# FFN1 of a macaron layer: the weight ring's hi halves moved by 64 bytes, and the down projections cut into two pieces of 384 tokens

## The chip, the cores and the metric

The kernel runs on one NeuronCore of a Trainium2 chip. The metric is the device time of one execution in microseconds (us): median 1112.95 us of three runs (1112.82 to 1113.49). Lower is better. TensorE multiplies matrices and accumulates in PSUM banks of 512 fp32 columns; VectorE (DVE), ScalarE (ACT) and GpSimd (POOL) work elementwise; SyncE (SP) issues the loads.

## What is computed

One hybrid backbone layer over 512 latent and 256 context tokens, model width 1024, feed-forward width 2816:

```
def swiglu(h, w1, w3, w2):
    return (jax.nn.silu(h @ w1) * (h @ w3)) @ w2

def ffn_sublayer(h_in, shift, scale, gate, norm_w, w1, w3, w2):
    h = modulate(rms_norm(h_in, norm_w), shift, scale)
    return h_in + 0.5 * gate * swiglu(h, w1, w3, w2)

x   = ffn_sublayer(x, ...norm1, ffn1)        # FFN1, latent tokens
ctx = ffn_sublayer(ctx, ...norm1, ffn1)      # FFN1, context tokens
...                                          # attention and spatial gating
x   = ffn_sublayer(x, ...norm3, ffn2)        # FFN2, latent tokens only
```

The nine shifts, scales and gates come from `silu(c) @ w_ada + b_ada`. All of it is fp32.

## The kernel before, in words

Each fp32 operand is held as two parts: hi (rounded to the multiplier's format) and lo (the rest). One product of a weight and an activation is three matmuls on TensorE, `mm3`: hi weight by hi activation, hi weight by lo, lo weight by hi. In the rows of the profile the weights are `oph` and `opl`, the normalised input of FFN1 is `hh` and `hl`, and the product silu·gate, the input of the down projection, is `gh` and `gl`.

FFN1 handles all 768 tokens together, ordered as two groups of 384 (256 latent and 128 context tokens each). The 22 feature tiles of 128 are made in turn. Tiles 0 and 1 are made in the prologue, 2 and 3 plainly (two 384-column halves), and 4 to 21 by a Winograd scheme of seven half-size products instead of eight (`Winograd.unit`; its operands are slices of hh, hl and the sums `u2`, `u3`, `u4`). Every product there is 12 matmuls of 384 columns. The down projection comes in four chunks of 5, 5, 6 and 6 feature tiles: the first three stand behind feature tiles 6, 10 and 16 (`DOWN1`, `after1`), the last one behind tile 21 (`last_mm`, in two halves of 384 already).

The weights come by DMA into raw tiles. ScalarE casts 512 columns to hi, VectorE subtracts to get lo; a pair of them is one of five slots (`OPS`) of a ring (`Stream.pair`). `Flow` keeps the order: `slot` first runs the evacuations left over from the product before, then gives back its ring slots, refills the ring and runs a filler (in the down stages two dot products of the modulation on VectorE, `ada_step`). From slot to slot the order on every engine is that in which the code is written.

`down_thirds` makes one output tile of 128 features at a time from three pieces of 256 tokens: the latent tokens of group 0, those of group 1, and the 2 × 128 context tokens. The first two fill one PSUM bank, the third a second one. VectorE adds the first bank into x (`evac_part`) while the third piece runs, and the second bank in the next slot. The last product ahead of each such stage (`cut`) has its last three matmuls split into 128 and 256 columns.

PSUM has eight banks: four under the name `mm`, and four that are either four `one` or two pairs `big`. A Winograd tile takes four `mm` when its number is even, four `one` when it is odd.

Each tile has a fixed place in SBUF. Of a partition's row, counted modulo 128 bytes: hh, hl, the sums u2 to u4 and all ten ring tiles start at 64; the g tiles of FFN1 start at 0. In FFN2 the ring is at 64 too, and most token blocks at 0.

Of the kernel before, what the change touches and what calls it, by code (L numbers as in the profile page):

```python
# [17 lines left out]
P = 128  # L18
# [10 lines left out]
CHUNKS1 = [5, 5, 6, 6]  # L29
DOWN1 = [6, 10, 16]  # L30
# [6 lines left out]
BLOCKS = 2  # L37
RAWS = 3
OPS = 5
GA, GB = (0, 384), (384, 384)  # L40

COL_B, COL_N1, COL_N2, COL_N3 = 0, 72, 80, 88
COL_QA, COL_KVA, COL_BS, COL_QN, COL_KN, COL_C = 96, 98, 99, 107, 108, 109
# [74 lines left out]
class Stream:  # L118


    def __init__(self, nc, raw_pool, op_pool, op_bufs, dram):
        self.pin = lambda i: i
        self.nc, self.raw_pool, self.op_pool, self.op_bufs, self.dram = nc, raw_pool, op_pool, op_bufs, dram

    def block(self, src, i, pool=None):
# [15 lines left out]
        return dst  # L141

    def pair(self):
        return [self.op_pool.tile([P, 512], F32R, tag=f"op{p}", bufs=self.op_bufs, name=f"op{p}_{self.nc.next_id()}") for p in "hl"]

    def operand(self, src, eng=None):
        return self.split([t[:, : src.shape[1]] for t in self.pair()], src, eng)
# [26 lines left out]
def layer_kernel(ctx: ExitStack, tc: tile.TileContext, xT, wfirst, wst, wada, wuq, wkpe, cols, wrope, vnw, rope, out):  # L174
    nc = Core(tc)
# [66 lines left out]
    fctx = ExitStack()  # L242
    fp = fctx.enter_context(tc.tile_pool(name="ffn1", bufs=2))
    cb = fp.tile([P, 2, D], F32, tag="cb", bufs=1, name="cb")
    gp = fctx.enter_context(tc.tile_pool(name="ffn1g", bufs=2))
    hfctx = ExitStack()
    hfp = hfctx.enter_context(tc.tile_pool(name="hf", bufs=1))
# [435 lines left out]
    gt = {}  # L683
# [60 lines left out]
        for p in range(2 * n):  # L744
            flow.todo.append(lambda p=p: want(p))

    def down_thirds(flow, f0, n, step):
        pairs, gone = [], 0
        for dt in range(NK):
            flow.slot(lambda: step(dt))  # L750
            while 4 * len(pairs) < dt * n + n:
                pairs.append(flow.take())
            pts = [mm(), mm()]
            for t in range(3):
                o = pts[0][:, 256 * t : 256 * t + 256] if t < 2 else two(pts[1][:, :256])
                for fi in range(n):
                    q, u = divmod(dt * n + fi, 4)
                    g = [a[:, 384 * t : 384 * t + 256] if t < 2 else two(a)[:, :, 256:384] for a in gt[f0 + fi]]
                    mm3(nc, o, [a[:, u * P : u * P + P] for a in pairs[q]], g, fi == 0, fi == n - 1)
                if t == 1:  # L760
                    evac_part(pts[0], dt, "lat", 512)

            def last(pt=pts[1], dt=dt):
                evac_part(pt, dt, "ctx", 256)
                yield

            flow.pend = [last()]
            flow.spent = (dt * n + n) // 4 - gone
            gone += flow.spent
# [36 lines left out]
        nc.scalar.copy(dst[0], src)  # L806
        nc.vector.tensor_sub(dst[1], src, dst[0].bitcast(F32))

    def prod(pb, A, Bk, n, first=True, cut=False):
        for i in range(4):  # L810
            s = slice(i * P, i * P + P)
            parts = ((256, n), (0, 256)) if cut and i == 3 else ((0, n),)
            for a, b in parts:
                mm3(nc, pb[:, a:b], (A[0][:, s], A[1][:, s]), (Bk[0][:, i, a:b], Bk[1][:, i, a:b]), first and i == 0,
                    i == 3 and a == 0, not first)

    class Winograd:

# [71 lines left out]
        def product(self, bank, blk, first, pend, step=None, cut=False):  # L890
            flow = self.flow
            a = flow.take()
            flow.slot(step or (lambda: None))
            prod(bank, a, self.blocks[blk], self.n, first, cut)
            flow.spent = 1
            flow.pend = [pend] if pend else []

        def open(self, f, step, f0=None, splits=()):
            n = self.n
            banks = [one() if f % 2 else mm() for _ in range(4)]  # L900
            banks = [banks[i] for i in (0, 1, 3, 2)]
            p1 = self.tmp("p1", n)

            def evac():
                nc.scalar.copy(p1, banks[0][:, :n])
                yield
                if f == f0:
                    for split_g in splits:
                        split_g()

            self.product(banks[0], "B11", True, evac(), step)
            return banks, p1

        def unit(self, f, hd, step):
            n, v = self.n, nc.vector
            banks, p1 = hd
            X, Y, Z, W = (b[:, :n] for b in banks)
            u2, u3 = self.tmp("u2", n), self.tmp("u3", n)
            sl = self.tmp("sl", n, self.sl_bufs)
            gh, gl = self.g_tile(f)  # L920

            def ev_sl():
                nc.scalar.activation(sl, X, AF.Silu)
                yield

            def ev_u2():
                v.tensor_add(u2, Y, p1)
                yield

            def ev_u2z():  # L930
                v.tensor_add(u2, Y, p1)
                yield
                v.tensor_add(Z, Z, u2)

            def ev_u3():
                nc.scalar.copy(u3, W)
                v.tensor_add(u3, Z, u3)
                yield

            def ev_lo():  # L940
                v.tensor_add(W, W, u2)
                v.tensor_mul(W, W, sl)
                yield
                g_split(W, gh[:, :n], gl[:, :n])

            def ev_hi(seeded=False):
                if not seeded:
                    v.tensor_add(Z, Z, u2)
                yield
                nc.scalar.activation(Z, Z, AF.Silu)  # L950
                v.tensor_mul(Z, Z, u3)
                g_split(Z, gh[:, n:], gl[:, n:])

            def ev_u3a():
                v.tensor_add(u3, W, u2)
                yield

            def ev_u3b():
                v.tensor_add(u3, Z, u3)
                yield  # L960

            nxt = None
            if f == self.late or f + 1 == NF:
                self.product(banks[1], "T2", True, ev_u2(), lambda: step(f, 0))
                self.product(banks[3], "T3", True, ev_u3a(), lambda: step(f, 1))
                self.product(banks[0], "B21", False, ev_sl(), lambda: step(f, 2))
# [12 lines left out]
            self.product(banks[2], "B22", False, ev_hi(seeded), cut=n > 256 and f in DOWN1)  # L979
            return nxt  # L980

        def run(self, flow, f0, after, step=lambda f, i: None, opening=None, splits=()):
# [6 lines left out]
            flow.slot()  # L989
            other_banks()  # L990

    def evac_part(pt, dt, g, n):
        sel, which = (lat, 0) if g == "lat" else (cxt, 1)
        v = sel(x, dt)
        nc.vector.scalar_tensor_tensor(v, two(pt[:, :n]), mod_g[0][which][:, dt : dt + 1], v, ALU.mult, ALU.add)

    ada = ada_rest()

    def ada_step(n=1):
        for _ in range(n):  # L1000
            next(ada, None)
# [3 lines left out]

    def after1(flow, f):
        for ci in ends1(f):
            down_thirds(flow, starts1[ci], CHUNKS1[ci], lambda dt: ada_step(2))

    def ada_up(f, i):  # L1010
        if f == NPLAIN1:
# [56 lines left out]
                yield  # L1068

    flow = Flow(OPS)  # L1070
    for f in range(NFIRST):
        g_tile(f)
    wino = Winograd(gp, 384, U_UP1, blocks, g_tile, 1, 4)
# [180 lines left out]
        pt = last_mm(0, dt)  # L1254
    assert next(consts, None) is None and len(lastp) == 2 * lastn
    hA = hB = None
    inw = [[] for _ in range(3)]

    def in_want(i, w):
# [670 lines left out]
    flat = lambda T: [t.rearrange("p k c -> p (k c)") for t in T]  # L1930
    sA, sB = SsqAcc(t3, 256, nc.vector), SsqAcc(t3, 256, nc.vector)
    homes = [[wpool.tile([P, 1024], F32R, bufs=1, name=f"w{w}{p}") for p in "hl"] for w in range(2)] + [flat(T3), flat(T4)]
    wpool.tile([P, 16], F32, bufs=1, name="pad_w")

    def w_hi(w):
        for i in (0, 512):
# [269 lines left out]
```

## Time and profile before

| | us |
|---|---|
| median of three runs | 1112.95 |
| span of the profiled execution (the only time that its profile gives) | 1110.9 |
| TensorE busy (its weight loads) | 1104.4 (1056.4) |
| VectorE, ScalarE, GpSimd busy | 882.9, 537.7, 308.9 |
| prologue with feature tiles 0 and 1 | 0 to 60.6 |
| feature tiles 2 to 21 and three down stages | 60.6 to 487.2 |
| of it the down stages | 139.9 to 180.7, 239.1 to 280.0, 367.5 to 416.5 |
| last down chunk of FFN1 | 487.2 to 538.1 |
| projections, attention, gating | 538.1 to about 770 |
| FFN2 | about 770 to 1110.9 |

A group row names line, engine, operation, output and inputs, shape and count, then busy time, the mean time of one in ns, and idle time before them. A row of the chain of waits gives the start, the time and the count of work that followed on without another releaser. Times of single matmuls include the part in which they overlap their neighbours; the distance from one start to the next is shorter. The granted TensorE clock is 1.0 throughout.

### The profile page before, as it was taken

The numbers are of one execution on the slowest core, as the hardware profiler recorded it, in microseconds if no ns is written. First come the engines' busy times: TensorE is split into PE (matmuls) and PEld (weight loads), VectorE is DVE, ScalarE is ACT, GpSimd is POOL, SyncE is SP. The second block draws the span as 40 slices with busy tenths as digits, with TensorE's granted clock in tenths as the row PEclk, the third lists the DMA queues.
The fourth block names the chain that finished last, engine by engine and source line by source line (L and its number), as shares of the span: only waits on it lengthen the run. The fifth ranks groups of instructions, "written<-read, shape, count | busy, mean of one in ns | idle before, by whom it ended". The sixth has DMA issues, their size and how long they took to land.

```text
span 1110.9 us, 19724 instructions
## 1 busy us (share of the span) xinstructions
PE 1104.4 (99%) x7616; PEld 1056.4 (95%) x7616; DVE 882.9 (79%) x1590; ACT 537.7 (48%) x1110; POOL 308.9 (28%) x268
## 2 busy tenths in 40 slices
PE   9999999999999999999999999999999999999998
PEld 7899999999999999999988889999999989898997
DVE  5779898888888778866756899978886969696884
ACT  6545422431444214444755559985554536353451
POOL 0003303312243023300008427750014425152330
PEclk9999999999999999999999999999999999999999
DMA  9721353344334765312242211003221422333302
GB/s 357 272 65 50 123 169 127 114 135 151 120 107 151 239 200 190 114 59 79 86 134 94 76 38 34 26 21 114 77 96 57 144 86 83 108 115 114 114 2 95
DMA packets 35678, 125.96 MB, mean 113 GB/s; under 512 B 3712, under 2 KB 10624, under 8 KB 30976
## 3 DMA queue, kind: packets, MB, share of 16 engines
q1 hardware_dynamic: 35440, 124.63, 33.1%
q8 instruction: 60, 0.98, 0.4%
q14 instruction: 34, 0.28, 0.1%
q10 hardware_dynamic: 144, 0.06, 0.0%
HBM read 122.58 MB, written 2.10 MB: 112 GB/s over the span
## 4 chain that ended last, share of the span: by engine, by line
PE 94%; DVE 3%; DMA 1%; ACT 1%; issue 0%; POOL 0%; SPq 0%; ACTq 0%; DVEq 0%; POOLq 0%
PE mm L59 55%; PE one L59 19%; PE big L59 8%; PE mm L169 2%; PE mm L170 2%; PE mm L168 2%; PE big L596 1%; PE mm L581 1%; DMA scale<-wada 1%; PE big L170 1%; PE big L168 1%; PE big L169 1%; PE mm L330 1%; DMA x<-xT 0%; DVE opl L59 0%
## 5 line engine op out<-in xcount | busy, mean ns | idle before, releaser
L59 DVE TENSOR_TENSOR opl<-block,oph 128x512 fp32r<-128x512 f32 x216 | 190.0, 888 | 29.8 <-ACT oph L59 27.4
L59 POOL TENSOR_TENSOR block<-block 128x512 f32<-128x512 f32 x69 | 104.1, 1509 | 380.2 <-DVE opl L59 377.6
L59 ACT CAST oph<-block 128x512 fp32r<-128x512 f32 x216 | 133.9, 622 | 109.0 <-PE mm L59 81.9
L59 PE MATMUL mm<-gh,oph 128*128 128x256 f32 (+2 forms) x573 | 176.7, 308 | 0.0
L59 PE MATMUL mm<-gl,oph 128*128 128x256 f32 (+2 forms) x573 | 176.4, 308 | 0.0
L59 PE MATMUL mm<-gh,opl 128*128 128x256 f32 (+2 forms) x573 | 176.4, 308 | 0.0
L59 DVE SCALAR_TENSOR_TENSOR x<-mm,g,x 128x512 f32<-128x512 f32 (+2 forms) x136 | 79.1, 601 | 47.4 <-PE mm L59 47.1
L59 PEld LDWEIGHTS mm<-gl,oph 128*128 128x128 f32 x573 | 107.6, 188 | 5.6
L59 PEld LDWEIGHTS mm<-gh,oph 128*128 128x128 f32 x573 | 107.6, 188 | 5.5
L59 PEld LDWEIGHTS mm<-gh,opl 128*128 128x128 f32 x573 | 107.6, 188 | 5.4
L59 ACT CAST oph<-raw 128x512 fp32r<-128x512 f32 x113 | 68.7, 621 | 77.5 <-PE mm L59 53.0
L59 DVE TENSOR_TENSOR opl<-raw,oph 128x512 fp32r<-128x512 f32 x113 | 77.6, 702 | 11.6 <-ACT oph L59 10.9
L59 POOL TENSOR_TENSOR block<-s,block 128x512 f32<-128x512 f32 x35 | 46.6, 1331 | 130.4 <-DVE opl L59 129.6
L59 PE MATMUL mm<-hh,oph 128*128 128x384 f32 (+2 forms) x195 | 65.2, 334 | 0.0
L59 PE MATMUL mm<-hl,oph 128*128 128x384 f32 (+2 forms) x195 | 64.8, 333 | 0.0
L59 PE MATMUL mm<-hh,opl 128*128 128x384 f32 (+2 forms) x195 | 64.8, 332 | 0.0
L59 DVE SCALAR_TENSOR_TENSOR junk<-raw,cb 128x1024 bf16<-128x1024 f32 x48 | 62.2, 1309 | 0.0
L59 POOL TENSOR_TENSOR s<-block 128x512 f32<-128x512 f32 x34 | 55.6, 1636 | 10.6 <-DMA block<-wst 10.6
L59 DVE SCALAR_TENSOR_TENSOR raw<-raw,cb 128x1024 f32<-128x1024 f32 x32 | 42.2, 1323 | 7.9 <-DMA raw<-wada 7.9
L59 PE MATMUL one<-hl,oph 128*128 128x384 f32 x144 | 48.1, 334 | 0.0
L59 PE MATMUL one<-hh,oph 128*128 128x384 f32 x144 | 48.1, 334 | 0.0
L59 PE MATMUL one<-hh,opl 128*128 128x384 f32 x144 | 48.1, 334 | 0.0
(711 smaller groups left out, 3382.8 us busy)
## 6 DMA issues: line engine op xcount, KB each, us to landing
raw<-wst SPq DMA_DIRECT2D x77, 512.0 KB, 3.9
block<-wst SPq DMA_DIRECT2D x36, 1024.0 KB, 5.0
raw<-wada SPq DMA_DIRECT2D x56, 512.0 KB, 4.3
scale<-wada SPq DMA_DIRECT2D x16, 512.0 KB, 9.0
x<-xT SPq DMA_DIRECT2D x5, 512.0 KB, 6.3
raw<-wfirst SPq DMA_DIRECT2D x8, 256.0 KB, 9.1
out<-x SPq DMA_DIRECT2D x7, 256.0 KB, 2.3
raw<-wuq SPq DMA_DIRECT2D x2, 384.0 KB, 5.1
```

The source lines that it names most:

```text
L59: return lambda *a, **k: self.tc.keep_in_program_order(f(*a, **k))
L168: nc.tensor.matmul(out, lh, rh, start=first, stop=False, skip_group_check=more)
L169: nc.tensor.matmul(out, lh, rl, start=False, stop=False, skip_group_check=more)
L170: nc.tensor.matmul(out, ll, rh, start=False, stop=last, skip_group_check=more)
L330: pin(nc.tensor.matmul(pa[q, :P], scw[:, kt, 2 - 2 * w : 34 - 2 * w], units[d][w][:, kt * P : kt * P + P], start=w == 0 and kt < 4, stop=w ...
L581: pin(nc.tensor.matmul(o, l[:, c], r, start=k == 0 and m == 0 and w == 0, stop=k == NK - 1 and m == 2, skip_group_check=True))
L596: pin(nc.tensor.matmul(two(pbs[i]), ops[k][lo][:, i * P : i * P + P], lat(r, k), start=False, stop=k == NK - 1 and m == 2, skip_group_chec ...
```

## The change

The five ring slots become two tiles, one for hi and one for lo, of which slots are slices. The hi tile is 16 elements (64 bytes) longer. With `st.lower = 16`, set ahead of feature tile 2's weights and unset behind FFN1, a hi slice starts 16 elements lower, which is 0 modulo 128 bytes; lo slices stay at 64. Three pads move what follows: the ring's own, one ahead of FFN1's g tiles (which now start at 64), and a longer one ahead of FFN2's kept weights (which stay at 64, 128 bytes lower). `down_thirds` becomes `down_halves`: two pieces of 384 tokens, one for each group, in the two banks of one `big`; both additions into x run in the next slot. The split of the last matmuls (`cut`) goes. Even Winograd tiles of FFN1 use two `big` pairs, odd ones the four `mm`.

```
     def pair(self):
-        return [self.op_pool.tile([P, 512], F32R, tag=f"op{p}", bufs=self.op_bufs, ...) for p in "hl"]
+        if not self.ring:
+            self.op_pool.tile([P, 48], F32, name="pad_ring")
+            self.ring = [self.op_pool.tile([P, 512 * self.op_bufs + n], F32R, name=f"op{p}") for p, n in (("h", 16), ("l", 0))]
+        o = self.pairs % self.op_bufs * 512
+        self.pairs += 1
+        return [t[:, a : a + 512] for t, a in zip(self.ring, (o + 16 - self.lower, o))]
...
+    fp.tile([P, 16], F32, bufs=1, name="pad_g")
     gp = fctx.enter_context(tc.tile_pool(name="ffn1g", bufs=2))
...
-    def down_thirds(flow, f0, n, step):
+    def down_halves(flow, f0, n, step):
...
-            pts = [mm(), mm()]
-            for t in range(3):
-                o = pts[0][:, 256 * t : 256 * t + 256] if t < 2 else two(pts[1][:, :256])
+            pt = big()
+            for h in range(2):
                 for fi in range(n):
                     q, u = divmod(dt * n + fi, 4)
-                    g = [a[:, 384 * t : 384 * t + 256] if t < 2 else two(a)[:, :, 256:384] for a in gt[f0 + fi]]
-                    mm3(nc, o, [a[:, u * P : u * P + P] for a in pairs[q]], g, fi == 0, fi == n - 1)
-                if t == 1:
-                    evac_part(pts[0], dt, "lat", 512)
-            def last(pt=pts[1], dt=dt):
-                evac_part(pt, dt, "ctx", 256)
+                    g = [a[:, 384 * h : 384 * h + 384] for a in gt[f0 + fi]]
+                    mm3(nc, pt[:, h, :384], [a[:, u * P : u * P + P] for a in pairs[q]], g, fi == 0, fi == n - 1)
+            def last(pt=pt, dt=dt):
+                for sel, which, o in ((lat, 0, slice(0, 256)), (cxt, 1, slice(256, 384))):
+                    v = sel(x, dt)
+                    nc.vector.scalar_tensor_tensor(v, pt[:, :, o], mod_g[0][which][:, dt : dt + 1], v, ALU.mult, ALU.add)
                 yield
...
-            parts = ((256, n), (0, 256)) if cut and i == 3 else ((0, n),)
-            for a, b in parts:
-                mm3(nc, pb[:, a:b], (A[0][:, s], A[1][:, s]), (Bk[0][:, i, a:b], Bk[1][:, i, a:b]), first and i == 0,
-                    i == 3 and a == 0, not first)
+            mm3(nc, pb[:, :n], (A[0][:, s], A[1][:, s]), (Bk[0][:, i, :n], Bk[1][:, i, :n]), first and i == 0, i == 3, not first)
...
-            banks = [one() if f % 2 else mm() for _ in range(4)]
+            if n > 256:
+                banks = [mm() for _ in range(4)] if f % 2 else bigs(4)
+            else:
+                banks = [one() if f % 2 else mm() for _ in range(4)]
...
     flow = Flow(OPS)
+    st.lower = 16
...
     hA = hB = None
+    st.lower = 0
...
-    wpool.tile([P, 16], F32, bufs=1, name="pad_w")
+    wpool.tile([P, 48], F32, bufs=1, name="pad_w")
```

On TensorE, at the entry to the first down stage (behind feature tile 6; `mm_1511` and `big_1391` are the banks of that tile's last product, `mm_1789` and `big_1622` those of output tile 0). Before:

```order
L59 MATMUL mm_1511<-hl,oph_1643 128x384
L59 MATMUL mm_1511<-hh,opl_1645 128x384
L59 MATMUL mm_1511<-hh,oph_1643 128x128
L59 MATMUL mm_1511<-hl,oph_1643 128x128
L59 MATMUL mm_1511<-hh,opl_1645 128x128
L59 MATMUL mm_1511<-hh,oph_1643 128x256
L59 MATMUL mm_1511<-hl,oph_1643 128x256
L59 MATMUL mm_1511<-hh,opl_1645 128x256
L59 MATMUL mm_1789<-gh_764,oph_1669 128x256
```

With the change:

```order
L58 MATMUL big_1391<-hl,oph 128x384
L58 MATMUL big_1391<-hh,opl 128x384
L58 MATMUL big_1391<-hh,oph 128x384
L58 MATMUL big_1391<-hl,oph 128x384
L58 MATMUL big_1391<-hh,opl 128x384
L58 MATMUL big_1622<-gh_748,oph 128x384
```

Six matmuls of 128 and 256 columns have become three of 384, and the down stage goes on in that width: 30 matmuls for an output tile of five feature tiles, where 45 stood before.

On VectorE, over the first output tile of that stage (`accc`, `accx` are sums of the modulation, `g_83` its gate, `opl` the next weights' lo part). Before:

```order
L59 SCALAR_TENSOR_TENSOR x<-mm_1789,g_83,x 128x2x256 [waits PE_49]
L59 SCALAR_TENSOR_TENSOR x<-mm_1791,g_83,x 128x2x128 [waits PE_49]
L59 TENSOR_TENSOR opl_1842<-raw_1765,oph_1840 128x512 [waits Activation_49]
L59 SCALAR_TENSOR_TENSOR junk_1849,accc<-raw_1846,cb 128x1024 [waits DMAHW7_49]
L59 TENSOR_SCALAR g_83<-accc,col 128x1 [waits DVE_49]
L59 SCALAR_TENSOR_TENSOR junk_1853,accx<-raw_1846,cb 128x1024
```

With the change:

```order
L58 SCALAR_TENSOR_TENSOR x<-big_1622,g_83,x 128x2x256 [waits PE_49]
L58 SCALAR_TENSOR_TENSOR x<-big_1622,g_83,x 128x2x128
L58 TENSOR_TENSOR opl<-raw_1602,oph 128x512 [waits Activation_49]
L58 SCALAR_TENSOR_TENSOR junk_1661,accc<-raw_1658,cb 128x1024 [waits DMAHW7_49]
L58 TENSOR_SCALAR g_83<-accc,col 128x1 [waits DVE_49]
L58 SCALAR_TENSOR_TENSOR junk_1665,accx<-raw_1658,cb 128x1024
```

The two additions into x keep their shapes and their place; the second no longer waits for TensorE on its own, since both banks are finished together.

More of the change, by code (lines that the diff above doesn't have):

```diff
@@ L39 @@
 OPS = 5
-GA, GB = (0, 384), (384, 384)
 COL_B, COL_N1, COL_N2, COL_N3 = 0, 72, 80, 88
@@ L122, in __init__ @@
         self.pin = lambda i: i
+        self.pairs, self.lower, self.ring = 0, 0, None
         self.nc, self.raw_pool, self.op_pool, self.op_bufs, self.dram = nc, raw_pool, op_pool, op_bufs, dram
@@ L143, in pair @@
     def pair(self):
-        return [self.op_pool.tile([P, 512], F32R, tag=f"op{p}", bufs=self.op_bufs, name=f"op{p}_{self.nc.next_id()}") for p in "hl"]
+        if not self.ring:
[4 more added lines that the diff above has]
+        return [t[:, a : a + 512] for t, a in zip(self.ring, (o + 16 - self.lower, o))]
     def operand(self, src, eng=None):
@@ L807, in split, with prod @@
         nc.vector.tensor_sub(dst[1], src, dst[0].bitcast(F32))
-    def prod(pb, A, Bk, n, first=True, cut=False):
+    def prod(pb, A, Bk, n, first=True):
         for i in range(4):
             s = slice(i * P, i * P + P)
-            parts = ((256, n), (0, 256)) if cut and i == 3 else ((0, n),)
-            for a, b in parts:
-                mm3(nc, pb[:, a:b], (A[0][:, s], A[1][:, s]), (Bk[0][:, i, a:b], Bk[1][:, i, a:b]), first and i == 0,
-                    i == 3 and a == 0, not first)
+            mm3(nc, pb[:, :n], (A[0][:, s], A[1][:, s]), (Bk[0][:, i, :n], Bk[1][:, i, :n]), first and i == 0, i == 3, not first)
     class Winograd:
@@ L888, in plan, with product @@
                 w = nxt
-        def product(self, bank, blk, first, pend, step=None, cut=False):
+        def product(self, bank, blk, first, pend, step=None):
             flow = self.flow
@@ L893, in product @@
             flow.slot(step or (lambda: None))
-            prod(bank, a, self.blocks[blk], self.n, first, cut)
+            prod(bank, a, self.blocks[blk], self.n, first)
             flow.spent = 1
@@ L978, in unit @@
             self.product(banks[3], "T4", False, ev_lo(), lambda: step(f, 3))
-            self.product(banks[2], "B22", False, ev_hi(seeded), cut=n > 256 and f in DOWN1)
+            self.product(banks[2], "B22", False, ev_hi(seeded))
             return nxt
@@ L990, in run @@
             other_banks()
[L992 to L995, printed above, removed]
     ada = ada_rest()
@@ L1007, in after1 @@
         for ci in ends1(f):
-            down_thirds(flow, starts1[ci], CHUNKS1[ci], lambda dt: ada_step(2))
+            down_halves(flow, starts1[ci], CHUNKS1[ci], lambda dt: ada_step(2))
     def ada_up(f, i):
```

## The prediction

> **What bounds the kernel now.** I read the head of the profile page first, then the waits of TensorE, then the chain of waits, cut to one stage at a time.
>
> ```profile
> span 1110.9 us, 19724 instructions
> PE 1104.4 (99%) x7616; PEld 1056.4 (95%) x7616; DVE 882.9 (79%) x1590; ACT 537.7 (48%) x1110; POOL 308.9 (28%) x268
> PE 94%; DVE 3%; DMA 1%; ACT 1%; issue 0%; POOL 0%; SPq 0%; ACTq 0%; DVEq 0%; POOLq 0%
> ```
>
> The chain that ended last is 94% TensorE. What TensorE waits for is small:
>
> ```profile
> PE mm L288 <- DVE epsc L223: 1.0, 1, 1.0
> PE mm L59 <- DVE u L59: 1.0, 3, 0.4
> PE big L588 <- ACT hh L59: 0.4, 1, 0.4
> ```
>
> None of these three is in the part of FFN1 that changes (the first and third lie in the prologue, the second in FFN2). So the time there is a number of matmuls times the distance from one start to the next, which I call the pitch. The durations in the group rows cannot give it, since neighbours overlap:
>
> ```profile
> L59 PE MATMUL one<-hl,oph 128*128 128x384 f32 x144 | 48.1, 334 | 0.0
> ```
>
> A 384-column matmul is shown as 334 ns, but the chain moves on by much less. A row of the chain is start, time and count of one unbroken run of matmuls, so time divided by count is the pitch. The chain, cut to single stages (first the three down stages, then one Winograd product of FFN1, then a 512-column stretch of FFN2):
>
> ```profile
> 140.41 40.25 PE mm L59 x355
> 239.78 40.12 PE mm L59 x354
> 368.14 48.28 PE mm L59 x426
> 110.76 8.32 PE one L59 x48
> 885.80 18.36 PE mm L59 x81
> ```
>
> The three down stages of 256 columns run at 40.25/355 = 113.4, 113.3 and 113.3 ns. A Winograd product of 384 columns runs at 8.32/48 = 173.3 ns, and 512 columns at 18.36/81 = 226.7 ns. From 384 to 512 columns that is 53.4 ns for 128 columns, so 384 columns stream for 160.0 ns and 256 for 106.7 ns. What stands above the stream is 13.3 ns for 384 and 512 columns, but only 6.7 ns for the 256 of the down stages.
>
> The same 256-column form does not always have that short gap:
>
> ```profile
> 49.97 10.44 PE mm L581 x87
> 855.32 5.44 PE mm L59 x48
> 864.95 5.65 PE one L59 x48
> ```
>
> The first row (prologue, moving operand hh or hl, weights from the ring) is 10.44/87 = 120.0 ns: a gap of 13.3 ns again. The other two are Winograd products of FFN2, 113.3 and 117.7 ns. What separates the first from the others is the place of the operands. As the program is laid out, hh, hl and all ring pairs start 64 bytes past a multiple of 128 bytes; the g tiles of FFN1 and FFN2's token blocks in the last two rows start on a multiple. So operands alike modulo 128 give 120.0 ns, and operands 64 bytes apart give 113.3 ns or, with the same operands' places and another history, 117.7 ns. All of FFN1's 384-column up products have moving operands and weights alike.
>
> **The change part by part.** (a) *The ring.* During FFN1 every hi half of a pair moves to a multiple of 128 bytes; lo halves and hh, hl, T blocks stay at 64 past. Of the three matmuls of a product (hi by hi, hi weight by lo, lo weight by hi), two now have weights 64 bytes away from the moving operand, one has them alike. No row of before has 384 columns in this mixed order. The nearest rows are the last chunk of FFN1, where g is 0 and the weights are all 64 past:
>
> ```profile
> 487.38 10.22 PE mm L59 x59
> 501.59 8.48 PE mm L59 x48
> ```
>
> They give 173.2 ns (weights in the ring) and 176.7 ns (weights in kept homes): at 384 columns, distance alone, held in every matmul, bought nothing. But the gap depends on history too, as 113.3 against 117.7 ns shows, and as the entry to a down stage shows (timeline of TensorE; start, modelled time, form):
>
> ```profile
> 139.20 0.22 PE L59 MATMUL mm<-hh,oph 128*128 128x128 f32 x1
> 139.48 0.34 PE L59 MATMUL mm<-hh,oph 128*128 128x256 f32 x1
> 139.90 0.28 PE L59 MATMUL mm<-gh,oph 128*128 128x256 f32 x1
> 140.49 0.28 PE L59 MATMUL mm<-gh,opl 128*128 128x256 f32 x1
> ```
>
> Five 256-column matmuls pass from 139.90 to 140.49, at 118 ns, before the 113.4 ns begins. So bounds for the new pitch are 166.7 ns (160.0 + 6.7, the short gap in all three) and 176.7 ns. I take the short gap in the two matmuls whose operands become 64 bytes apart and the long one in the third: (2 × 166.7 + 173.3)/3 = 168.9 ns. This is an estimate; the 256-column rows are nearest to it in kind of operand, the 487.38 row in width, and the order with one differing matmul in three is nearest to neither.
>
> The Trainium skill, TensorE: Matmul & The Clock Gate, section "Step-by-step: what each phase is for", says that TensorE reads moving operand and weights through two independent ports, so that loading the next weights takes nothing from the running matmul; by it no move of an address would change the pitch. The Trainium skill's section "Back-to-back issue gap" on the same page gives columns/2.4 + 2.5 ns, 109.2 and 162.5 ns for 256 and 384. The trace agrees with neither: 113.3 against 120.0 ns for one form, and 173.3 ns. By that formula in both layouts the edit (c) alone would count, 384 × (2 × 162.5 − 3 × 109.2) ns = −1.0 us, an estimate.
>
> (b) *The up products.* Two plain feature tiles are 2 × 96 matmuls and 18 Winograd tiles are 18 × 84, together 1704 of 384 columns. At 168.9 instead of 173.3 ns: −7.5 us.
>
> (c) *The down projections.* 8 output tiles × 16 feature tiles × 3 = 384 groups; each had three 256-column matmuls and now has two of 384. Before 1152 × 113.3 ns = 130.6 us, after 768 × 168.9 = 129.7 us: −0.9 us. At the old 173.3 ns it would be 133.1 us, +2.5 us, so this edit pays only through the ring.
>
> (d) *The split entry.* Three times the last three 384-column matmuls ahead of a down stage were cut into 128 and 256 columns. From 139.20 to 139.90 they take 0.70 us where three whole ones take 0.52; with 0.02 for the five longer ones after, 3 × 0.2 = −0.6 us.
>
> (e) *The last chunk.* Its 120 matmuls with ring weights: 120 × (168.9 − 173.2) ns = −0.5 us. Its 168 with kept weights lie between 173.2 and 176.7 ns in both layouts, ±0.6 us; I take 0.
>
> (f) *Evacuation and banks.* VectorE's two additions into x per output tile stay, 256 and 128 columns twice; only the first now waits for the whole tile instead of two thirds of it. It is read one output tile later than it is needed again at the earliest, some 30 matmuls or 5 us. VectorE is the engine with least room in a down stage:
>
> ```profile
> 140.49:180.72 40.23, 40.23 (x357) 40.23 (x356) 37.75 (x70) 6.51 (x12) 6.03 (x3) 1.00 0.45 145
> ```
>
> VectorE is busy 37.75 of 40.23 us. The stage becomes 240 × 168.9 ns = 40.5 us, so the cover holds; at 166.7 ns it is 40.0 us and still holds by 2.3 us. Ring slots are released by the same last readers and stay full as far ahead: 0. Banks 4 to 7 now serve even Winograd tiles and the down stages, 0 to 3 odd ones; whoever follows a down stage uses the other four: 0.
>
> (g) *FFN2 and between.* Ring, g tiles and kept weights keep their places modulo 128: 0. Its cover is only that history falls out alike. About 1400 matmuls of FFN2 run at 113.3 ns; at 117.7 they would cost +6.2 us, and the some 470 slower ones could gain 2 us.
>
> Sum: −7.5 − 0.9 − 0.6 − 0.5 = −9.5 us. Against the profiled span that is 1110.9 − 9.5 = 1101.4 us. The median of the runs, 1112.95 us, lies 2.0 us above the span, which I keep: **1103.4 us**.
>
> **The rivals.** *All three matmuls take the short gap* (166.7 ns). For it: in the down stages the 113.3 ns holds for every one of the three. Against it: one matmul in three has its operands alike. Ups 1704 × 6.6 = −11.3, downs 128.0 − 130.6 = −2.6, entries −0.6, last chunk −0.8: −15.3 us, 1097.6 us.
>
> *The layout does not matter at 384 columns* (173.3 ns). For it: the 487.38 row, 64 bytes apart and no faster. Against it: 256 columns do react. The two independent ports of the Trainium skill (TensorE: Matmul & The Clock Gate, the section named above) would end here too. The time: downs +2.5, entries −0.6, so +1.9 us, 1114.9 us. Here the ring's shift does nothing.
>
> *The mixed order lengthens the pitch* (the other side). The 501.59 row shows a pitch of 176.7 ns at 384 columns, with weights 64 bytes away from g, entered through a change of weights between layouts; the mixed ring changes layout twice in every product, and could stay there. Against it: 59 matmuls with the same distance stayed at 173.2 ns. Ups 1704 × 3.4 = +5.8, downs 135.7 − 130.6 = +5.1, last chunk +0.4, entries −0.6: +10.7 us, 1123.7 us. With p as the new pitch the whole change is 2592 p − 446.7 − 0.6 us (446.7 = 1824 × 173.3 + 1152 × 113.3 ns), so it costs time from p = 172.6 ns on, and more than 0.2% from 173.4 ns.
>
> *FFN2 falls out of step* as in (g): up to +6.2 us on any of these; alone with the forecast it would leave −3.3 us, 1109.6 us.
>
> **How the numbers follow.** Two of three short 0.38, all short 0.24, no effect 0.20, longer pitch 0.12, FFN2 out of step 0.06. A measurement of this kernel can tell about 0.2%, 2.2 us, from no change. Faster: 0.38 + 0.24 and nothing of the rest taken for certain, 0.62. No effect ends 0.3 us under that bound, so 0.15 of its 0.20 is within it; the remaining 0.05, the longer pitch and the 0.06, where FFN2 may turn any of the others, make 0.23 slower. The likeliest case alone reaches from 1101 to 1107 us. The range takes in all short with 2.6 us for FFN2's longer pitches turning fast, and no effect with 2 us to spare: 1095 to 1117 us.
>
> **What would show it.** The chain rows of the Winograd products: 8.11 us for 48 matmuls if two of three are short, 8.00 if all are, 8.32 if none. The down stages: 40.5 us where 240 matmuls run, against 40.8 us for the 360 of before. The starts of single matmuls in one product: 167, 167, 173 ns in turn. FFN2 from 770 us on should last as long as before within 2 us. The prediction is wrong if the 384-column pitch is at or over 173.3 ns, if TensorE shows a new wait in the down stages for VectorE or a bank, or if the gain lies outside FFN1.

## The result, and the profile after

The changed kernel takes 1192.12 us (median of 4 runs, 1189.83 to 1193.6) against 1112.88 us for the kernel before on the same chip: a ratio of 1.0709, 95% interval 1.0693 to 1.0724. It is 79 us slower; the forecast was 1103.4 us with 1117 us as the upper end.

The head of the page of the changed kernel, and the shares of its chain of waits by engine:

```profile
span 1189.4 us, 18955 instructions
PE 1135.6 (95%) x7223; PEld 1078.8 (91%) x7223; DVE 885.3 (74%) x1590; ACT 537.5 (45%) x1110; POOL 306.7 (26%) x268
PE 85%; DVE 9%; ACT 2%; issue 2%; DMA 2%; POOL 0%; SPq 0%; ACTq 0%; DVEq 0%; POOLq 0%
```

Before, the chain was 94% TensorE and 3% VectorE. TensorE issues 393 instructions fewer and is yet busy 31 us longer, and VectorE, with the same 1590 instructions, now stands in the chain for 9%. So two things have happened: TensorE waits, and its matmuls take longer.

Where: the windows of the changed kernel by stage (first column the stretch and its length, then busy time and count of TensorE, of its weight loads, VectorE, ScalarE, GpSimd, then the granted clock, the DMA share and GB/s). The rows are the first down stage, the up products between it and the second, the last up products, and all behind FFN1:

```profile
152.80:198.80 46.00, 46.00 (x253) 46.00 (x254) 37.55 (x69) 7.15 (x13) 6.19 (x3) 0.96 0.40 127
198.90:268.70 69.80, 59.69 (x324) 57.77 (x322) 49.16 (x77) 25.74 (x50) 17.64 (x13) 0.98 0.30 106
...
477.90:552.80 74.90, 64.54 (x337) 62.62 (x336) 49.05 (x79) 26.03 (x51) 18.77 (x14) 0.93 0.32 110
...
617.20:1189.40 572.20, 567.22 (x3923) 529.48 (x3921) 450.98 (x825) 314.94 (x670) 203.26 (x192) 1.00 0.25 83
```

The kernel before, between its first two down stages and behind FFN1:

```profile
180.70:239.10 58.40, 58.40 (x341) 58.40 (x340) 47.28 (x77) 26.05 (x50) 18.17 (x13) 1.00 0.36 126
...
538.10:1110.90 572.80, 568.34 (x3928) 530.76 (x3926) 450.00 (x825) 315.26 (x670) 202.80 (x192) 1.00 0.25 83
```

572.2 against 572.8 us: behind FFN1 nothing is lost. Inside it, TensorE is idle for 10.1 and 10.4 us of the two stretches of up products, in the down stage not at all, and the granted clock, which was 1.00 throughout before, is 0.93 to 0.98 and returns to 1.00 behind.

What TensorE waits for in the changed kernel (total, times, longest):

```profile
PE big L58 <- DVE gl L58: 23.9, 9, 3.1
PE big L58 <- DVE big L58: 14.7, 8, 2.0
PE big L58 <- ACT sl L58: 5.7, 9, 1.0
```

All are waits of a product into a `big`, eight or nine times each: once per even Winograd tile (4, 6, ... 20). With three more in FFN1, of 2.7 us together, they are 29 waits; the kernel before has none of them. The chain through one of them, tile 8, shows the three places (start, time, what):

```profile
216.41 1.42 PE big L58 x8
...
217.85 0.50 ACT sl L58
...
218.39 2.38 PE big L58 x12
...
220.80 0.56 DVE u L58
221.35 0.69 DVE opl L58
222.05 0.48 DVE big L58
...
222.57 2.39 PE big L58 x12
224.96 2.12 PE mm L58 x12
...
229.88 0.56 DVE big L58
...
230.47 0.57 DVE big L58
231.03 0.60 DVE opl L58
231.63 0.52 DVE gl L58
...
232.19 3.92 PE big L58 x12
```

`Winograd.open` gives X and Y the one pair, Z and W the other. T2 goes into Y right after B21 into X, and at 217.85 TensorE stands until ScalarE has read X (`sl`). T3 goes into W right after T2, during which Z is free; but VectorE adds `u2` onto Z only then, behind `u` and the next weights' `opl`, and TensorE stands from 220.77 to 222.57. B22 goes into Z right after T4 into W, and TensorE stands until W has been added to, multiplied, and split (`gl`), to 232.19. In none of these three does TensorE want the bank that is being read: it wants its partner in the pair.

The last row shows the second loss. Twelve matmuls of 384 columns take 3.92 us there, and 8.43 us is what 48 take in an odd tile:

```profile
120.16 8.43 PE mm L58 x48
```

That is 327 against 175.6 ns. TensorE's timeline behind the third wait has the starts 320 ns apart for eleven matmuls:

```profile
232.19 0.52 PE L58 MATMUL big<-hh,oph 128*128 128x384 f32 x1 [3.02 <-DVE gl L58]
232.51 0.52 PE L58 MATMUL big<-hl,oph 128*128 128x384 f32 x1
...
235.39 0.52 PE L58 MATMUL big<-hl,oph 128*128 128x384 f32 x1
...
235.94 0.34 PE L58 MATMUL mm<-hh,oph 128*128 128x384 f32 x1
```

384 columns stream in 160 ns at the full clock (worked out in the prediction); 320 ns is twice that, half the rate. The granted clock (third number from the end) of three stretches of 3.41 us, one after the other, says the same:

```profile
229.00:232.41 3.41, 0.39 (x2) 0.22 (x2) 3.10 (x5) 1.10 (x2) 2.00 (x2) 1.00 0.00 0
232.41:235.82 3.41, 3.41 (x12) 3.41 (x12) 0.00 (x0) 0.00 (x0) 0.00 (x0) 0.50 0.00 0
235.82:239.24 3.42, 3.42 (x21) 3.42 (x20) 2.05 (x4) 2.00 (x4) 1.30 (x1) 1.00 0.00 0
```

There are eleven such bursts in FFN1 of the changed kernel and none in the kernel before. And third, the undisturbed pitch is 175.6 ns, longer than the 173.3 ns of before.

From start to start of neighbouring matmuls, less one pitch each, the 29 waits add up to 51.6 us. A burst costs half of its length, some 1.7 us, eleven of them 19 us. The rest of the 79 us, some 8 us, should be the pitch. Each of the three was then tested by itself.

### The profile page after: what moved, and what is told of

Read it like the earlier page. It is cut to its first block, busy times and chain, and to the rows that moved or that the text cites. A ratio compares the mean times of both kernels' runs of the same rounds, so it can differ in the third digit from the quotient of the medians.

```text
span 1189.4 us, 18955 instructions
## 1 busy us (share of the span) xinstructions
PE 1135.6 (95%) x7223; PEld 1078.8 (91%) x7223; DVE 885.3 (74%) x1590; ACT 537.5 (45%) x1110; POOL 306.7 (26%) x268
## 4 chain that ended last, share of the span: by engine, by line
PE 85%; DVE 9%; ACT 2%; issue 2%; DMA 2%; POOL 0%; SPq 0%; ACTq 0%; DVEq 0%; POOLq 0%
PE mm L58 40%; PE big L58 29%; PE one L58 7%; DVE opl L58 2%; PE mm L175 1%; PE mm L174 1%; PE mm L173 1%; DVE big L58 1%; PE big L602 1%; PE mm L587 1%; DMA scale<-wada 1%; ACT oph L58 1%; DVE u L58 1%; PE mm L336 0%; DVE gl L58 0%
## 5 line engine op out<-in xcount | busy, mean ns | idle before, releaser
L58 PE MATMUL big<-hh,oph 128*128 128x384 f32 (+1 forms) x200 | 72.2, 361 | 25.4 <-DVE gl L58 23.9
L58 PE MATMUL big<-gl,oph 128*128 128x384 f32 x256 | 87.4, 341 | 0.0
L58 PE MATMUL big<-gh,opl 128*128 128x384 f32 x256 | 86.9, 340 | 0.0
L58 PE MATMUL big<-gh,oph 128*128 128x384 f32 x256 | 86.8, 339 | 0.0
L58 DVE SCALAR_TENSOR_TENSOR x<-mm,g,x 128x512 f32<-128x512 f32 (+1 forms) x88 | 50.5, 595 | 40.2 <-PE mm L58 40.2
L58 PE MATMUL big<-hl,oph 128*128 128x384 f32 (+1 forms) x200 | 71.6, 358 | 0.0
L58 PE MATMUL big<-hh,opl 128*128 128x384 f32 (+1 forms) x200 | 71.1, 355 | 0.0
L58 PE MATMUL mm<-gh,oph 128*128 128x512 f32 (+2 forms) x189 | 70.6, 374 | 0.0
L58 PE MATMUL mm<-gl,oph 128*128 128x512 f32 (+2 forms) x189 | 70.5, 373 | 0.0
L58 PE MATMUL mm<-gh,opl 128*128 128x512 f32 (+2 forms) x189 | 70.4, 373 | 0.0
L58 PE MATMUL mm<-hh,oph 128*128 128x384 f32 x192 | 65.1, 339 | 0.0
```

Source lines behind the costliest of these rows:

```text
L58: return lambda *a, **k: self.tc.keep_in_program_order(f(*a, **k))
```

## The experiments

Theory A is that account: a product waits for whoever reads either bank of its pair (some 52 us), long waits are followed by matmuls at half rate (some 19 us), and the mixed layout has the longer pitch (some 8 us). Rival B puts the waits down to the ring, now two long tiles with one shifted; rival C puts the half rate down to the new places of the operands.

**Other partners.** One line of `open`; X is paired with W and Y with Z, so that no product of an even tile (but in tile 4, whose order differs) follows its partner's evacuation:

```
-            banks = [banks[i] for i in (0, 1, 3, 2)]
+            banks = [banks[i] for i in (0, 2, 3, 1)]
```

> The changed kernel with one edit: in a Winograd tile the four banks X, Y, Z, W are put into the two pairs as X with W and Y with Z, where the change puts X with Y and Z with W. Theory A (a product waits for everybody who still reads either bank of its pair; of the 79 us, some 52 are these waits, some 19 are matmuls at half rate behind the long ones, some 8 the longer pitch): in an even tile no product now follows the evacuation of its partner at once, so the three waits per tile go and with them the half rate. Left are the pitch (+7.9 us), one wait in tile 4 (about 1 us) and up to 1 us at each of the three entries into a down stage, whose first pair is X with W: 1112.9 + 7.9 + 1 + 2.5 = 1124 us, granted clock 1.00. Rival B (the ring as two long tiles, or its shift, makes TensorE wait for weights): the waits stay, 1185 to 1192 us. Rival C (the half rate comes of the new places of the operands and not of the waits): only the waits go, 1124 + 19 = 1143 us with the clock still under 1.

Measured 1128.45 us (1128.36 to 1129.67), ratio to the kernel before 1.0139 (1.0124 to 1.0154), clock 0.998. TensorE's longest wait in FFN1 (the others come to 1.8 us):

```profile
PE big L58 <- DVE u L58: 4.3, 1, 4.3
```

The waits of all other even tiles have gone, and the bursts with them but for one behind the wait of 4.3 us; rivals B and C fall. The miss of 4 us is tile 4: its product B21 into X waits for `u3`, which reads W, and VectorE comes to it late. The chain of that place shows what stands ahead:

```profile
100.49 1.70 DVE opl L58
102.19 1.55 DVE hl L58
...
104.39 0.60 DVE opl L58
...
105.85 0.56 DVE u L58
```

The lo parts of the next weights and of the last token block are queued on VectorE in this slot.

With X and Z, Y and W as partners (`(2, 0, 3, 1)`) two products follow their partner's evacuation, both times a short one:

> As the run with X and W paired, but X with Z and Y with W. Theory A: two of an even tile's products now follow their partner's evacuation, but both times a short one: T1 into Z waits for ScalarE's copy of X (0.7 us), T3 into W for VectorE's sum that reads Y (0.7 to 1.5 us). Nine tiles give 13 to 20 us, and no wait over 2 us stands ahead of a product, so no half rate: 1124 + 17 = 1141 us, between 1137 and 1146. Rival B (ring): 1185 to 1192 us. Rival C (half rate from the places): 1160 us.

Measured 1145.48 us (1143.79 to 1147.25), ratio 1.0284 (1.0267 to 1.0301). The waits lie where they were expected, at T3 into W behind VectorE's sum `u2`, which reads Y, once per tile:

```profile
PE big L58 <- DVE u L58: 18.4, 9, 4.4
```

ScalarE's copy of X was in time, so the other one did not appear. But three bursts at half rate stand behind waits of 2.1, 2.4 and 4.5 us, so "no wait over 2 us" and with it "no half rate" was wrong.

**No shift.** `st.lower = 0` in FFN1, all else as changed:

> The changed kernel with the ring's hi halves not shifted (lower stays 0; the ring is still two long tiles, the pairs and the two pieces of 384 stay). Theory A: pitch 173.3 ns instead of 175.6 for 2592 matmuls, -6.0 us; the waits and the half rate stay: 1186 us. Rival B, as far as it is the shift that makes TensorE wait: down to 1115 us; as far as it is the two long tiles: 1186 us like theory A, but then the run with X and W paired has the waits too. Rival C (half rate from the new places): the clock returns to 1.00 and 19 us more go, 1167 us.

Measured 1193.71 us (1191.48 to 1195.02), ratio 1.0721 (1.0705 to 1.0737), clock 0.975. The waits are the same 51.7 us, so it isn't the shift that makes TensorE wait, and the pitch is back at 173.3 ns. But the 6 us that this is worth do not show: this run has half rate for seventeen times 3.41 us (fifteen bursts, two of them of double length), where the changed kernel has eleven. I had taken their number as given.

**Pairs alone, on the kernel before.** Odd tiles get their banks as two pairs; ring, places, thirds stay:

```
-            banks = [one() if f % 2 else mm() for _ in range(4)]
+            banks = (bigs(4) if n > 256 else [one() for _ in range(4)]) if f % 2 else [mm() for _ in range(4)]
```

> The kernel before with one edit: odd Winograd tiles of FFN1 take their four banks as two pairs (X with Y, Z with W) instead of four single ones; ring, places, down projections in thirds and everything else stay as before. Theory A: eight odd tiles wait as the even ones of the changed kernel do (0.7 + 2.0 + 2.9 = 5.6 us each), the last one, in its other order, some 3.7 us, together 49 us, and behind each long wait ten matmuls at half rate (1.4 us each time): 13 us. 1112.9 + 62 = 1175 us, between 1165 and 1185, with a clock under 1. Rivals B and C (the ring or the places do it): 1113 us, clock 1.00.

Measured 1192.46 us (1184.33 to 1194.28), ratio 1.0697 (1.066 to 1.0734), clock 0.977. This edit alone costs as much as the whole change. The waits have the same three places:

```profile
PE big L59 <- DVE gl L59: 24.2, 9, 3.2
PE big L59 <- DVE big L59: 18.4, 8, 3.9
PE big L59 <- ACT sl L59: 4.6, 8, 0.6
```

They come to 52.2 us; the half rate took sixteen times 3.41 us and cost 27 us, where I had allowed 13 us.

**No pairs.** Four single banks for every Winograd tile and two for an output tile of the down stages leave layout and pieces alone (VectorE's two additions become four, hidden in the stage):

```
-                banks = [mm() for _ in range(4)] if f % 2 else bigs(4)
+                banks = [mm() if f % 2 else one() for _ in range(4)]
...
-            pt = big()
+            pts = [one(), one()]
```

> The changed kernel with four single banks for every Winograd tile and two single banks for an output tile of the down stages (VectorE's two additions into x become four smaller ones); the ring's shift and the two pieces of 384 stay. This leaves the layout and the pieces alone. Theory A': no wait and no half rate is left, and the pitch is the 175.5 ns that the runs with pairs show between their waits: 2592 x 175.5 - 447.3 = +7.6 us, 1120.5 us. Rival D (the long pitch comes with the waits, each of which upsets the rhythm for a while): 173.3 ns, +1.9 us, 1114.8 us.

> As the run with single banks, and the ring's hi halves not shifted: every moving operand of FFN1 and all weights start at 64 modulo 128. This leaves the two pieces of 384 (and the missing split at the entries) alone. Theory A': pitch 173.3 ns, 2592 x 173.3 - 447.3 = +1.9 us, 1114.8 us. Rival D: the same as with the shift, within 1 us.

> As the run with single banks, but hi and lo halves of the ring are both lowered by 64 bytes: in FFN1 all weights start at 0 and all moving operands at 64 modulo 128, the distance that has 113.3 instead of 120.0 ns at 256 columns. If only a mixed order costs and an even distance is neutral at 384 columns (as the 173.2 ns of the last chunk before says): 1114.8 us. If an even distance is worth the short gap at 384 columns too: 166.7 ns, 1097.7 us. If an even distance costs as in the kept homes of the last chunk before (176.7 ns): 1123.7 us.

> The kernel before with the ring as two long tiles and its hi halves lowered during FFN1; banks, thirds and the split at the entries as before, g tiles still at 0. Theory A': no new wait; the up products go from 173.3 to 175.5 ns, 1704 x 2.2 = +3.7 us, and the thirds, whose hi weights now lie alike with g and whose lo weights 64 bytes away, go from 113.3 ns to between 113.3 and 120.0 ns, 0 to +7.7 us: 1116.6 to 1124.6 us, middle 1120. Rival D (no pitch change without waits): 1113 us for the ups, and at most the thirds' +7.7 us.

| | median us | ratio to before | four up products (x48), us | up pitch ns | down pitch ns |
|---|---|---|---|---|---|
| before | 1113.17 | 1 | 8.32 | 173.3 | 113.3 (256 columns) |
| single banks, hi shifted | 1120.66 | 1.0067 (1.0053 to 1.0081) | 8.43 | 175.6 | 175.6 |
| single banks, no shift | 1115.05 | 1.0017 (1.0008 to 1.0025) | 8.32 | 173.3 | 173.3 |
| single banks, hi and lo shifted | 1122.34 | 1.0083 (1.0069 to 1.0096) | 8.43 | 175.6 | 173.4 |
| before with hi shifted | 1122.13 | 1.008 (1.0067 to 1.0092) | 8.43 | 175.6 | 117.9 (256 columns) |

The pitches are rows of the chain of waits. Four up products of 12 matmuls each, with hi shifted and without a shift:

```profile
112.82 8.43 PE mm L58 x48
```

```profile
112.11 8.32 PE mm L58 x48
```

And the inside of the first down stage with hi shifted, without a shift, with both shifted, and last in the kernel before with hi shifted:

```profile
141.97 41.08 PE one L58 x234
```

```profile
141.92 40.21 PE one L58 x232
```

```profile
141.93 40.22 PE one L58 x232
```

```profile
140.45 41.63 PE mm L59 x353
```

The three runs with single banks have one new wait, of 1.2 us at the start of tile 4; the kernel before with hi shifted has none. All four have the granted clock 1.00. So the layout costs by itself, without any wait, and rival D (the long pitch comes with the waits) falls: 7.5 us for shift and pieces together, of which 1.9 us are the pieces with that wait and 5.6 us the shift. Within a product the starts are 173, 177.5 and 176 ns apart in turn in the mixed order. The shift hurts the thirds too: g lies at 0, and the hi weights now alike, so 113.3 becomes 117.9 ns. With both halves shifted the up products keep 175.6 ns, and it matters nothing to them where lo lies; the down products, with the same places modulo 128 as the up products, come to 173.4 ns on average with single steps of 169 to 178 ns. No place that was tried gave 384 columns a pitch under the 173.2 to 173.3 ns of before.

The 1122.34 us of the run with both shifted are not the price of FFN1's layout, though. FFN1 ends 2.1 us earlier there than with hi alone shifted; what follows it takes 575.6 against 571.9 us, where the shift is off again and, by its pads, the edit has only moved what lies behind the ring by 128 bytes. The same stretch of FFN2, mostly 512 columns wide, with hi shifted and with both:

```profile
891.66 23.46 PE mm L58 x111
```

```profile
890.77 24.06 PE mm L58 x111
```

So a pitch seems to change even where the places modulo 128 bytes are left alone; why was not tested.

**Filling the wait.** Is it the idle time that brings the half rate? Ahead of B22 in each even tile of the changed kernel, 16 or 8 matmuls without use go into a bank of the next tile that isn't begun yet:

```
+            for _ in range(16 if fill is not None else 0):
+                nc.tensor.matmul(fill[:, :384], a[0][:, :P], self.blocks[blk][0][:, 0, :384], start=True, stop=True)
             prod(bank, a, self.blocks[blk], self.n, first)
```

> The changed kernel with 16 extra matmuls of 384 columns ahead of the last product (B22 into Z) of each even Winograd tile; they multiply that product's own weights into a bank of the next tile that is not begun yet, and the result is overwritten. They run in the place where TensorE waits 2.5 to 3.2 us for the evacuation of W, take 16 x 175 ns = 2.8 us of it, and change no wait of another engine. Theory A (a wait in which TensorE stands idle for about 2 us or more is followed by some ten matmuls at half rate): those bursts go, about 110 matmuls x 145 ns = 16 us, though TensorE has 144 matmuls more to do: 1192.1 - 16 = 1176 us, between 1172 and 1180, clock over 0.99. Rival E (the half rate has nothing to do with the idle time): 1192 to 1195 us.

> As the run with 16 extra matmuls, with 8: they cover 1.4 us, and 1.1 to 1.8 us of the wait stay idle. Theory A with a limit near 2 us in one stretch: the bursts behind this wait go as with 16, 1176 us. Theory A with the share of idle time over some 10 us (the two earlier waits of a tile, 0.7 and 2.0 us, count too): about half of them stay, 1184 us. Rival E: 1192 us.

Measured 1184.45 us (1180.38 to 1186.32), ratio 1.0629 (1.0609 to 1.0649), with 16, and 1182.08 us (1177.71 to 1186.54), ratio 1.0619 (1.0594 to 1.0644), with 8, between the two forms of theory A that were on record for it (1176 and 1184 us). More work on TensorE, and less time: rival E (the half rate has nothing to do with the idle time) falls. But only half of the gain came. With 16 no burst stands behind the filled wait any longer; seven now stand behind the wait ahead of it, of 2 us, as in tile 8:

```profile
221.96 0.44 PE L58 MATMUL big<-u3h,oph 128*128 128x384 f32 x1 [1.81 <-DVE big L58]
222.24 0.34 PE L58 MATMUL big<-u3l,oph 128*128 128x384 f32 x1
222.41 0.39 PE L58 MATMUL big<-u3h,opl 128*128 128x384 f32 x1
222.60 0.52 PE L58 MATMUL big<-u3h,oph 128*128 128x384 f32 x1
222.92 0.52 PE L58 MATMUL big<-u3l,oph 128*128 128x384 f32 x1
```

Here the first three matmuls behind the wait still have the full rate, and the half rate begins 0.6 us after the wait's end: it isn't the wait's end that starts it. I took the last step at half rate of every burst of the seven runs that have any. Counted modulo 3413.3 ns, in each run they lie within some 300 ns, about the length of one matmul (in the changed kernel at 60 to 273, eleven of them over 430 us of the run). The trace's own record of the granted clock agrees: in each run every stretch at half clock is 3.413 us long or twice that, and the beginnings lie on such a grid within some 5 ns. So the clock is set anew at ticks 3.413 us apart. Laying each run's ticks over its waits and adding up the idle time between two ticks separates the cases: of the stretches that themselves ran at the full clock, all with 1.94 us idle or more are followed by one at half clock (54), and none with 1.86 us or less (158, of which 45 had over 1 us). The two figures hold for ticks laid 0.1 us ahead of the record's beginnings; laid upon them, the lowest with a burst is 1.87 us and the highest without is 1.88 us. The border is some 1.9 us, and no sharper than that. A wait of 2 us brings a burst if it falls between two ticks, and none if a tick cuts it: behind waits of 1.94 to 2.26 us, 21 of 39 had one.

The Trainium skill, TensorE: Matmul & The Clock Gate, section "What's actually happening", says that TensorE's clock is either full or half, set by a monitor that looks at windows of 3413 ns which run freely, and is halved after a window in which TensorE was idle. The traces agree with the window to its last digit. In its section "HAM oscillation — how this bites in real kernels" the same page warns of idle gaps over 3.4 us. The traces differ there: some 1.9 us of idle time in one window are enough.

With that, each run can be added up from the run with single banks and the same layout (spans 1119.0 us with the shift, 1113.3 us without, 1110.9 us for the kernel before): its waits (less the 1.2 us that the runs with single banks have too), 1.71 us for each window at half clock, and the 175.6 ns for each extra matmul.

| | waits us | windows at half | extra matmuls us | sum | span |
|---|---|---|---|---|---|
| the change | 50.4 | 11 | | 1188.2 | 1189.4 |
| X with W | 5.7 | 1 | | 1126.4 | 1126.7 |
| X with Z | 21.1 | 3 | | 1145.2 | 1145.5 |
| no shift | 50.5 | 17 | | 1192.9 | 1193.2 |
| pairs on the kernel before | 52.2 | 16 | | 1190.5 | 1191.2 |
| 16 filled in | 26.5 | 7 | 25.3 | 1182.8 | 1184.2 |
| 8 filled in | 38.2 | 2 | 12.6 | 1173.2 | 1175.9 |

Five sums come within 1.2 us of the span; the two filled runs take 1.4 and 2.7 us longer than theirs, and why stays open.

That kernels with many such waits scatter by 3.5 to 10 us from run to run, and those with one or none by less than 2 us, would follow from it: where the ticks fall differs from run to run. Nothing was run to show that alone.

**Two single terms.** The kernel before without the split of the last matmuls ahead of a down stage, and with FFN2's g tiles moved to 0:

> The kernel before without the split of the last three matmuls ahead of a down stage. By term (d) of the prediction: -0.6 us, 1112.4 us. Rival: the first 256-column matmuls of the stage then fall into the longer pitch (118 instead of 113 ns for many more than five of them, as the run with the shifted ring shows 118 ns for whole stages): three stages of 355 x 4.5 ns give up to +4.8 us, 1118 us.

> The kernel before with FFN2's g tiles moved from 64 to 0 modulo 128 bytes, so that the 501 matmuls of 512 columns (226.7 ns, gap 13.3 ns, operands alike) and the last ones of 256 have operands 64 bytes apart. If the short gap belongs to 256 columns alone and an even distance at other widths is neutral: 1113.2 us. If 512 columns take the short gap (220.0 ns): -3.3 us, 1109.9 us. If they lengthen as 384 columns do (by 1 to 3 ns): +0.5 to +1.5 us, 1114 us.

Without the split: 1112.01 us (1111.96 to 1113.02), ratio 0.9992 (0.9983 to 1.0001), which the times alone cannot tell from no change. The chain can. The first down stage with its neighbours in the kernel before, and without the split:

```profile
135.72 45.16 PE mm L59 x387
```

```profile
135.62 44.96 PE mm L59 x384
```

0.20 us less, and 0.20 us less in the second and third too: 0.6 us in all, and the 113.3 ns inside stay: (44.96 − 24 × 0.1733)/360. FFN2's g tiles at 0: 1113.66 us (1113.36 to 1114.47), ratio 1.0007 (0.9998 to 1.0016). The same stretch of the down projection in the kernel before and with g moved:

```profile
883.45 23.46 PE mm L59 x111
```

```profile
883.78 23.65 PE mm L59 x111
```

So 512 columns take no short gap at that distance either; of the three widths only 256 columns have shown one. No version tried beats the kernel before by more than the measurement can tell.

## Why the prediction was wrong, point by point

**(f) Evacuation and banks: the step that failed.** "Banks 4 to 7 now serve even Winograd tiles and the down stages, 0 to 3 odd ones; whoever follows a down stage uses the other four: 0." I asked only whether the next user of a bank finds it free. In an even tile it is the same tile that uses the pair, two products in a row, and a pair is one tile for the waits. Put at 0, it measured 1192.12 − 1120.66 = 71.5 us. The prediction named "a new wait in the down stages for VectorE or a bank" as what would prove it wrong; the wait came, but in the up products. In the down stages the pair cost nothing, as said: TensorE is busy 46.00 of 46.00 us in the first. None of the four rivals was a wait inside a tile; the 0.23 for slower was spread over the pitch and FFN2.

**The granted clock** was taken as 1.0 in both kernels. It is a result of the waits: some 19 of the 71.5 us.

**(a) The ring's pitch: wrong in sign.** "(2 × 166.7 + 173.3)/3 = 168.9 ns" became 175.6 ns, within the bounds (166.7 to 176.7) and near the rival with 0.12, *the mixed order lengthens the pitch*. The error was to carry the short gap of 256 columns over to 384 against the 487.38 and 501.59 rows, the only rows of 384 columns with the operands 64 bytes apart, which had shown 173.2 and 176.7 ns. They were nearest in width, and no run shows the short gap at their width. (The rows of 48 matmuls, which the prediction calls one product, are four; the pitch read from them is not touched.)

**(b), (c), (e), the sum.** The formula held. With 175.6 ns the prediction's 2592 p − 447.3 gives +7.9 us, 1120.8 us; the run with single banks took 1120.66 us. With 173.3 ns it gives +1.9 us, 1114.9 us; the run without the shift took 1115.05 us. The hit to 0.2 us is in part luck: 1.2 us of both runs are the wait at tile 4, which is in no term, so the terms themselves are too high by about that much together. Some 0.5 us of it lies behind FFN1, which took 571.9 and 572.0 us in these two profiled executions against 572.5 us before; where the rest lies isn't known.

**(d) The split entry: right,** −0.20 us three times, as estimated.

**(g) FFN2: right,** 572.2 against 572.8 us behind FFN1.

**The rivals.** *All short* and the forecast fall with the 175.6 ns. *The layout does not matter* falls: the layout costs 5.6 us. The two independent ports (the Trainium skill, TensorE: Matmul & The Clock Gate, "Step-by-step: what each phase is for") would make the pitch the same in all the runs with single banks; it is 173.3 or 175.6 ns with nothing changed but the place of the weights, so the measurement decides against taking that page to mean that places are free.

## What to carry to other kernels

When banks are joined into one tile, list for every product what reads its partner at that moment, in the order in which the products are written: here a change of partners alone took 64 of the 79 us away. Price a wait of TensorE twice, by its own length and, where close to 2 us or more of idle time can fall into one window of 3.4 us, by another 1.7 us. And carry a gap over only between rows of the same width: what held for 256 columns held for neither 384 nor 512.

## What the runs showed of the hardware that was not expected

- The clock is halved for a whole window of 3413.3 ns, on a grid that runs through the execution, after a window with 1.94 us idle or more, and never after one with 1.86 us or less (some 1.9 us, as the place of the tick is known to 0.1 us). In a burst 384 columns take 320 ns.
- With all moving operands at 64 modulo 128 bytes and the hi weights at 0, 384 columns take 173, 177.5 and 176 ns in turn, whether lo weights lie at 0 or 64; alike they take 173.3 ns. Yet the down products with all weights at 0 and g at 64 average 173.4 ns, in steps of 169 to 178 ns. So places modulo 128 bytes alone don't settle the pitch, and at 512 columns the move by 128 bytes shows the same (24.06 against 23.46 us for 111 matmuls); what else does stays open.
- At 256 columns all weights 64 bytes away from g give 113.3 ns; hi alike and lo away give 117.9 ns, for every one of the three.
